# Four idle products in the opening, and the cumulated decays of both mixers by halves of the tokens

## The chip, the core and the metric

The program runs on one core of a Trainium2 chip. TensorE (PE, with its weight loads as PEld) multiplies into PSUM, VectorE (DVE), ScalarE (ACT) and GpSimd (POOL) work element by element, and SyncE (SP) issues most of the transfers from HBM. [...] The metric is the time of one execution in microseconds (us), the median of the runs.

## The reference, cut to what matters

A trunk of two layers works on 512 tokens of width 1024. Each layer modulates its input by a vector computed from `c` (adaLN), runs a mixer of gated linear attention and retention side by side, and then a channel mixer (dense in layer 0, eight experts in layer 1). The change touches the opening of layer 0, where the first modulation is made, and in both layers the cumulated decays `b` of the gated linear attention.

```python
cond = jax.nn.silu(c)
for layer in range(DEPTH):
    mod = (cond @ ada_w[layer] + ada_b[layer])[:, None, :]
    sh1, sc1, g1, sh2, sc2, g2 = jnp.split(mod, 6, axis=-1)
    h = rms_norm(x, norm_mix_g[layer]) * (1.0 + sc1) + sh1
    x = x + g1 * hybrid_mixer(h, positions, w_in[layer], ...)
    ...

def hybrid_mixer(h, ...):
    proj = (h @ w_in).astype(F32)
    gq, gk, gv, gr, ga, rq, rk, rv, rg = jnp.split(proj, ...)
    log_a = jax.nn.log_sigmoid(ga @ w_alpha + b_alpha) / GLA_TAU
    o_g = gla_core(gq * GLA_DK ** -0.5, gk, gv, log_a)      # in chunks of 64 tokens
    ...

def gla_core(q, k, v, log_a):
    b = jnp.cumsum(log_a, axis=2)
    b_last = b[:, :, -1:]
    eb, enb = jnp.exp(b), jnp.exp(-b)
    q_f, k_f = q * eb, k * enb
    q_b, k_b = q * enb, k * eb
    ...
```

## The kernel before, in words

Every weight matrix is read as f32 and split into two f16 halves (`split`: ACT writes `hi`, DVE writes `lo`), and every product of an activation with a weight is three f16 products (`mm3`, lines 221 to 223). The raw tiles stand in a ring of three buffers, the halves in rings of five.

**Opening (lines 1413 to 1438, `ada_first`).** The tokens are transposed (`px`), the scale of their norm is spread over the partitions (`prb`, line 400), and the scale and shift vectors of layer 0 are made from 8 MB of `ada_w`, in two halves of 512 columns, j = 1 (scale) before j = 0 (shift). A block of 128 rows of `ada_w` either goes through DVE, which adds it up in `acc` (lines 266 and 268), or through PE as a product with one column of output (`pr`, line 256), as the table `HOW` says. Products with one moving column bring the sum into columns (`pm`, lines 260 and 270), and DVE writes `mod` (line 273). From `mod` and the normalised tokens ACT makes `hh_m` and an f32 copy `u_m` (line 437), and DVE makes `hl_m` (line 438), for the eight blocks k of 128 features: blocks 0 to 3 need the first halves of scale and shift, blocks 4 to 7 the second ones.

**First products (`first`, lines 540 to 568).** For each k, PE multiplies into four banks of keys and queries (`pf_k`, `pf_q`) and into the bank of the gate's 16 columns (`pf_ga`, line 554). ACT then copies the four banks (`rawk`, `rawq`, line 568) and the gate (`gt`, line 560).

**The gate's chain (lines 560 to 607).** PE transposes `gt` into `pgt` (line 563), ACT copies it to `ga` (line 564), PE multiplies by the small matrix `wal` into two banks `pz`, one for each half of the tokens (line 578), ACT takes Abs, Exp and Ln of each (lines 582 to 586, with a load of the function table ahead of Exp and of Ln), and DVE makes the log decays, `es[0]` and `es[1]` (called `lge` in the trace, line 588), of 256 tokens each. Eight f32 products with a triangular matrix make the cumulated decays (`pbs`, line 596), and eight with two columns the chunks' ends (`pe`, line 597). ACT exponentiates them into `eb` and `enb`, which DVE needs for the keys and queries of the first step of the attention.

**Beside it.** `project_v` (line 510 on) makes the values `gv`: four tiles of 128 tokens, 24 f16 products each (96 in all, lines 221 to 223), which need nothing of the gate's chain. Also on ACT in this stretch: the sine and cosine of the rotary tables (`sinT`, `cosT`, lines 466 to 469) and the halves of later weights.

**What sets the order.** The program is written as straight code, but a scheduler of the framework decides the order of the instructions on each engine. PSUM has eight banks in two pools by tag: `at` with three, `pj` with five. During `first` all five `pj` banks are taken (four of keys and queries, one of the gate), and each tile of `gv` needs a `pj` bank. In the orders shown below, `pj` tiles are first written in the order in which the code asks for them.

Of the kernel before, what the change touches and what calls it, by code (L numbers as in the profile page):

```python
# [15 lines left out]
AF = mybir.ActivationFunctionType  # L16
ALU = mybir.AluOpType

P = 128
# [3 lines left out]
NT = T // P  # L23
# [95 lines left out]
def trunk(ctx, tc, a, out):  # L119
# [11 lines left out]
    def psum(name, tag="at", dt=F32):  # L131
        return ps_pool.tile([P, 512], dt, name=name, tag=tag, bufs=dict(at=3, pj=5)[tag])
# [20 lines left out]
    def scratch(name, dt=F32):  # L153
        return p1.tile([P, T], dt, name=name, tag="tmp", bufs=4)
# [73 lines left out]
    def ada_sum(l, j, c0, n, terms, scale):  # L228

        pm = psum(f"pm{l}_{j}_{c0}")  # L230
        for i in range(n // P):
            for m, (x, y) in enumerate(terms):
# [4 lines left out]
                                       (XS, 1.0, SCL)[j % 3] * scale, bcol[:, b0:b0 + n // P],  # L237
                                       op0=ALU.mult, op1=ALU.add)

    def ada_first(j, half, stage, how):  # L240

        if (0, j) not in mods:
            mods[0, j] = sb.tile([P, KC], F32, name=f"mod0_{j}")
        c0 = j * D + half * 512
        view, raw = kview(a["ada_w"][0][:, c0:c0 + 512]), []
        for i in range(2):
            r = stage.tile([P, 4, 512], F32, name=f"ada0_{j}_{half}_{i}", tag="ada", bufs=STG)
            last_dma[:] = [nc.sync.dma_start(r, view[:, i * 4:i * 4 + 4])]  # L250
            raw += [r[:, k] for k in range(4)]
        pm, acc, rows = psum(f"pm0_{j}_{half}"), None, [k for k in range(KC) if how[k] == "R"]
        if rows:
            pr = psum(f"pr0_{j}_{half}", "pj")[0:1]
            for k in rows:
                nc.tensor.matmul(pr, cond[:, k:k + 1], raw[k], start=(k == rows[0]), stop=(k == rows[-1]))
            row = scratch(f"row{j}_{half}")[0:1]
            nc.scalar.copy(row, pr)
            for i in range(4):
                nc.tensor.matmul(pm[:, i:i + 1], row[:, i * P:(i + 1) * P], ones[0:1, 0:1], start=(i == 0), stop=False)  # L260
        for k in range(KC):
            if how[k] == "V":
                c = cond[:, k:k + 1]
                if acc is None:
                    acc = stage.tile([P, 512], F32, name=f"acc{j}_{half}", tag="acc", bufs=2)
                    nc.vector.tensor_scalar(acc, raw[k], c, None, op0=ALU.mult)
                else:
                    nc.vector.scalar_tensor_tensor(acc, raw[k], c, acc, op0=ALU.mult, op1=ALU.add)
        for i in range(4):
            nc.tensor.matmul(pm[:, i:i + 1], acc[:, i * P:(i + 1) * P], ones[:, 0:1],  # L270
                             start=(not rows and i == 0), stop=(i == 3))
        b0, d0 = j * KC + half * 4, half * 4
        nc.vector.scalar_tensor_tensor(mods[0, j][:, d0:d0 + 4], pm[:, 0:4], (XS, 1.0)[j],
                                       bcol[:, b0:b0 + 4], op0=ALU.mult, op1=ALU.add)
# [214 lines left out]
    def mixer(l, hh, hl, ws, sp, ga_bank=None, tokens=None):  # L489
# [99 lines left out]
        la = [es[t // 2][:, (t % 2) * 256:(t % 2 + 1) * 256] for t in range(NT)]  # L589
        tri = con("tri")  # L590
        pe = psum(f"pe{l}")
        for p in range(2):
            pbs = psum(f"pbs{l}_{p}")
            for t in range(NT):
                w = la[t][:, p * P:(p + 1) * P]
                nc.tensor.matmul(pbs[:, t * P:(t + 1) * P], w, tri[:, 0:P], start=True, stop=True)
                nc.tensor.matmul(pe[:, p * 8 + 2 * t:p * 8 + 2 * t + 2], w, tri[:, P:P + 2],
                                 start=True, stop=True)
            nc.scalar.activation(eb[p], pbs, AF.Exp)
            nc.scalar.activation(enb[p], pbs, AF.Exp, scale=-1.0)  # L600
        ex = tl("ex", (P, 2, NT, 2))
        nc.scalar.activation(ex, pe[:, 0:16], AF.Exp)
        exx = tl("exx", (P, 2, NT - 1))
# [934 lines left out]
```

## Time and profile before

| | |
|---|---|
| median of 3 runs | 1371.9 us (1366.15 to 1373.17) |
| profiled execution, its own time | 1369.26 us |
| its span, first to last instruction | 1367.5 us |
| granted TensorE clock, mean | 0.984 |
| PE busy | 1318.8 us, 96% of the span |
| PEld / DVE / ACT / POOL busy | 924.9 / 1007.8 / 690.1 / 166.9 us |
| mean DMA rate | 205 GB/s |

The profiled execution lies 2.6 us below the median, and 1.8 us of it lie outside the span. A busy share is an average over stages, so what the change can give or take is read from the stretches that it touches: the first 95 us for layer 0, and the stretch from 660 to 690 us for layer 1. [...] In a row of the timeline the bracket at the end is the idle time of the engine just before, and what ended it; rows of one form that follow each other are merged.

### The profile page before, as it was taken

Reading aid. Unit: us, or ns where it says so; the run is one execution under the profiler, and the core shown is the slowest. Engines: PE = TensorE matmul, PEld = TensorE weight load, DVE = VectorE, ACT = ScalarE, POOL = GpSimd, SP = SyncE. Lnnn points to the kernel's source line nnn. Section 1 sums busy time; section 2 is a strip of 40 time slices with the busy share of each in tenths; the row PEclk is TensorE's granted clock in tenths of the full one; section 3 lists DMA queues with packets and bytes.
Section 4 is the critical chain, followed back from the end, with each engine's and each line's share of the span. In section 5 each row is a group of like instructions: output and inputs, shape, how many; then the busy total and the mean of one; then the engine's idle time right before and its main releaser. Section 6 shows DMA issues by size and latency. Waiting matters only on the chain.

```text
span 1367.5 us, 28435 instructions
## 1 busy us (share of the span) xinstructions
PE 1318.8 (96%) x11761; PEld 924.9 (68%) x11761; DVE 1007.8 (74%) x1823; ACT 690.1 (50%) x1107; POOL 166.9 (12%) x177
## 2 busy tenths in 40 slices
PE   5999999999999999999999999899999999999985
PEld 3455555574444444468655464599999999999983
DVE  6869977767778873236277875798988988978673
ACT  3762333444333432226632333577777877777563
POOL 1010100011122110002000401400000000000652
PEclk8999999999999999999999999999999999999997
DMA  9864643327768753324222200199999999989941
GB/s 343 287 205 135 206 134 101 114 63 218 247 226 294 229 189 116 111 82 139 94 93 92 68 1 1 35 379 383 360 312 353 360 308 364 361 290 353 318 155 64
DMA packets 163389, 279.78 MB, mean 205 GB/s; under 512 B 6224, under 2 KB 82012, under 8 KB 163252
## 3 DMA queue, kind: packets, MB, share of 16 engines
q1 hardware_dynamic: 149172, 229.01, 49.1%
q0 software_dynamic: 13936, 48.61, 10.9%
q8 instruction: 94, 1.54, 0.5%
q14 instruction: 43, 0.35, 0.1%
q10 hardware_dynamic: 144, 0.26, 0.1%
HBM read 271.80 MB, written 6.06 MB: 203 GB/s over the span
## 4 chain that ended last, share of the span: by engine, by line
PE 86%; DVE 6%; DMA 3%; ACT 2%; issue 1%; SPq 1%; POOL 0%; DVEq 0%; ACTq 0%; POOLq 0%
PE u L222 6%; PE u L223 6%; PE u L221 6%; PE eu L1176 5%; PE eu L1179 5%; PE eu L1177 5%; PE ed L1179 3%; PE ed L1177 3%; PE ed L1176 3%; PE pg L1198 2%; PE pd_None L223 2%; PE pd_None L222 2%; PE pd_None L221 2%; PE pj_gate L221 2%; PE pj_gate L222 2%; PE pj_gate L223 2%
## 5 line engine op out<-in xcount | busy, mean ns | idle before, releaser
L222 PE MATMUL u<-hl_f,hi_w 128*128 128x512 f16 (+1 forms) x384 | 137.5, 361 | 0.1
L223 PE MATMUL u<-hh_f,lo_w 128*128 128x512 f16 (+1 forms) x384 | 137.6, 361 | 0.0
L221 PE MATMUL u<-hh_f,hi_w 128*128 128x512 f16 (+1 forms) x384 | 135.2, 361 | 0.2 <-ACT hh_f L421 0.2
L203 ACT ACTIVATE hi_w<-raw_w 128x512 f16<-128x512 f32 (+1 forms) x136 | 72.9, 604 | 100.0 <-PE u L222 63.0
L204 DVE SCALAR_TENSOR_TENSOR lo_w<-raw_w,hi_w 128x512 f16<-128x512 f32 (+1 forms) x136 | 83.9, 671 | 37.2 <-ACT hi_w L203 37.0
L308 DVE SCALAR_TENSOR_TENSOR acc<-ada,conds,acc 128x512 f32<-128x512 f32 x140 | 104.9, 749 | 3.4 <-DMA ada<-in_ada_w 0.2
L294 POOL DMA_DIRECT2D ada<-in_ada_w x80 | 56.9, 712 | 347.8 <-DVE acc L308 320.9
L223 PEld LDWEIGHTS <-lo_w 128*128 128x128 f16 x604 | 59.1, 98 | 54.3 <-issue 0.3
L221 PEld LDWEIGHTS <-hi_w 128*128 128x128 f16 x604 | 59.2, 98 | 53.5 <-issue 0.2
L222 PEld LDWEIGHTS <-hi_w 128*128 128x128 f16 x604 | 59.0, 98 | 52.8
L1366 POOL DMA_INDIRECT y<-ybuf,rows x16 | 26.3, 1643 | 394.9 <-DMA raw_e7moe_w<-in_moe_w 388.8
L222 PE MATMUL pd_None<-al,hi_w 128*128 128x512 f16 x132 | 50.0, 379 | 0.0
L223 PE MATMUL pd_None<-ah,lo_w 128*128 128x512 f16 x132 | 50.0, 379 | 0.0
L221 PE MATMUL pd_None<-ah,hi_w 128*128 128x512 f16 x132 | 50.0, 379 | 0.0
L221 PE MATMUL pj_gate<-hh_m,hi_gate 128*128 128x512 f16 x128 | 48.5, 379 | 0.8 <-ACT g L766 0.8
L223 PE MATMUL pj_gate<-hh_m,lo_gate 128*128 128x512 f16 x128 | 48.5, 379 | 0.0
L222 PE MATMUL pj_gate<-hl_m,hi_gate 128*128 128x512 f16 x128 | 48.5, 379 | 0.0
L204 DVE SCALAR_TENSOR_TENSOR lo_e7moe_w<-raw_e7moe_w,hi_e7moe_w 128x2048 f16<-128x2048 f32 (+3 forms) x21 | 38.4, 1838 | 9.2 <-ACT hi_e7moe_w L203 6.3
L204 DVE SCALAR_TENSOR_TENSOR lo_e5moe_w<-raw_e5moe_w,hi_e5moe_w 128x2048 f16<-128x2048 f32 (+1 forms) x18 | 37.8, 2112 | 8.8 <-ACT hi_e5moe_w L203 8.6
L204 DVE SCALAR_TENSOR_TENSOR lo_e2moe_w<-raw_e2moe_w,hi_e2moe_w 128x2048 f16<-128x2048 f32 (+1 forms) x18 | 37.9, 2112 | 7.4 <-ACT hi_e2moe_w L203 7.1
L204 DVE SCALAR_TENSOR_TENSOR lo_e3moe_w<-raw_e3moe_w,hi_e3moe_w 128x2048 f16<-128x2048 f32 (+1 forms) x18 | 37.9, 2112 | 6.5 <-ACT hi_e3moe_w L203 6.3
L1198 PE MATMUL pg<-oneh,ht 128*128 128x284 f16 (+3 forms) x256 | 40.4, 295 | 2.1 <-DVE oneh L1191 2.1
(572 smaller groups left out, 4115.5 us busy)
## 6 DMA issues: line engine op xcount, KB each, us to landing
ada<-in_ada_w POOLq DMA_DIRECT2D x80, 512.0 KB, 5.0
raw_w<-in_ffn_w SPq DMA_DIRECT2D x26, 1024.0 KB, 6.5
raw_e1moe_w<-in_moe_w SPq DMA_DIRECT2D x12, 1024.0 KB, 8.0
raw_e2moe_w<-in_moe_w SPq DMA_DIRECT2D x12, 1024.0 KB, 6.5
raw_e3moe_w<-in_moe_w SPq DMA_DIRECT2D x12, 1024.0 KB, 8.1
raw_e4moe_w<-in_moe_w SPq DMA_DIRECT2D x12, 1024.0 KB, 7.4
raw_e5moe_w<-in_moe_w SPq DMA_DIRECT2D x12, 1024.0 KB, 7.1
raw_e6moe_w<-in_moe_w SPq DMA_DIRECT2D x12, 1024.0 KB, 7.4
```

Source lines behind the costliest of these rows:

```text
L203: nc.scalar.mul(hi, raw, WS)
L204: nc.vector.scalar_tensor_tensor(lo, raw, WS, hi, op0=ALU.mult, op1=ALU.subtract)
L221: nc.tensor.matmul(dst, wh, xh, start=first, stop=False)
L222: nc.tensor.matmul(dst, wh, xl, start=False, stop=False)
L223: last_mm[:] = [nc.tensor.matmul(dst, wl, xh, start=False, stop=last)]
L294: nc.gpsimd.dma_start(r, view[:, k:k + 2])
L308: op = nc.vector.scalar_tensor_tensor(acc, x, c, acc, op0=ALU.mult, op1=ALU.add)
L1176: nc.tensor.matmul(dst, wh[:, s], x1, start=(first and i == 0), stop=False)
L1177: nc.tensor.matmul(dst, wh[:, s], x2, start=False, stop=False)
L1179: nc.tensor.matmul(dst, wl[:, s], x1, start=False, stop=(last and i == len(ws) - 1))
L1198: nc.tensor.matmul(pg[:, 0:W], ht[j][t][d // 4][:, d % 4 * P:(d % 4 + 1) * P], oneh[:, t], start=(t == 0), stop=(t == NT - 1))
L1366: nc.gpsimd.indirect_dma_start(out=y, out_offset=None, in_=ybuf[half], in_offset=bass.IndirectOffsetOnAxis(ap=rows[:, i, t:t + 1], axis=0))
```

## The change

A function `idle` multiplies the identity by a tile of 512 columns in f32 and writes a `pj` bank that nobody reads. It is called four times, all in layer 0: on the finished `acc` of the first halves of scale and shift (`idle_a1`, `idle_a0`), on the last block of `ada_w` of the first row product (`idle_r0`), and on `es[0]` (`idle_g`). The products of the cumulated decays, which went through p (two groups of 128 channels) and in it through the four token tiles, now go through the halves of the tokens first, so that the first half of them reads `es[0]` alone; both `pbs` banks are asked for ahead of the loop, and the exponentials follow it. This holds for both layers; `idle_g` is called in layer 0 alone, between the halves.

```diff
+    def idle(name, x):
+
+        nc.tensor.matmul(psum(f"idle_{name}", "pj"), ident, x, start=True, stop=True)
+
     def ada_first(j, half, stage, how):
...
             for k in rows:
                 nc.tensor.matmul(pr, cond[:, k:k + 1], raw[k], start=(k == rows[0]), stop=(k == rows[-1]))
+            if half == 0:
+                idle(f"r{j}", raw[rows[-1]])
             row = scratch(f"row{j}_{half}")[0:1]
...
             nc.tensor.matmul(pm[:, i:i + 1], acc[:, i * P:(i + 1) * P], ones[:, 0:1],
                              start=(not rows and i == 0), stop=(i == 3))
+        if half == 0:
+            idle(f"a{j}", acc)
...
         pe = psum(f"pe{l}")
+        pbs = [psum(f"pbs{l}_{p}") for p in range(2)]
+        for j in range(2):
+            for p in range(2):
+                for t in (2 * j, 2 * j + 1):
+                    w = la[t][:, p * P:(p + 1) * P]
+                    nc.tensor.matmul(pbs[p][:, t * P:(t + 1) * P], w, tri[:, 0:P], start=True, stop=True)
+                    nc.tensor.matmul(pe[:, p * 8 + 2 * t:p * 8 + 2 * t + 2], w, tri[:, P:P + 2],
+                                     start=True, stop=True)
+            if l == 0 and j == 0:
+                idle("g", es[0])
         for p in range(2):
-            pbs = psum(f"pbs{l}_{p}")
-            for t in range(NT):
-                w = la[t][:, p * P:(p + 1) * P]
-                nc.tensor.matmul(pbs[:, t * P:(t + 1) * P], w, tri[:, 0:P], start=True, stop=True)
-                nc.tensor.matmul(pe[:, p * 8 + 2 * t:p * 8 + 2 * t + 2], w, tri[:, P:P + 2],
-                                 start=True, stop=True)
-            nc.scalar.activation(eb[p], pbs, AF.Exp)
-            nc.scalar.activation(enb[p], pbs, AF.Exp, scale=-1.0)
+            nc.scalar.activation(eb[p], pbs[p], AF.Exp)
+            nc.scalar.activation(enb[p], pbs[p], AF.Exp, scale=-1.0)
```

The scheduler orders much of layer 0 anew. Three places matter here. (Line numbers of the changed program are 4 to 12 higher.)

**PE, end of the first products of layer 0.** In the program before, the products of `gv` (`pv_gv`) follow the last product of the gate (`pf_ga`) directly:

```order
L554 MATMUL pf_ga_None<-gate_6_368,hh_m_400 128x32
L554 LDWEIGHTS hl_m_401
L554 MATMUL pf_ga_None<-gate_6_368,hl_m_401 128x32
L221 LDWEIGHTS hh_m_282
L221 MATMUL pv_gv_0_709<-hi_gv_0_687,hh_m_282 128x512
L222 LDWEIGHTS hh_m_282
L222 MATMUL pv_gv_0_709<-lo_gv_0_688,hh_m_282 128x512
```

The chain's own products `pgt` stood 31 products of `gv` further down, `pz` another 23 and `pbs` another 30. In the changed program:

```order
L562 MATMUL pf_ga_None<-gate_6_374,hl_m_407 128x32
L571 MATMUL pgt_None<-cst,gtNone_607 32x128 x4
L586 MATMUL pz_0_636<-wal_433,ga_437 128x256 x2
L586 MATMUL pz_1_637<-wal_433,ga_437 128x256 x2
L605 MATMUL pbs_0_653<-cst,lge_0_642 128x128
L606 MATMUL pe_652<-cst,lge_0_642 128x2
L605 MATMUL pbs_0_653<-cst,lge_0_642 128x128
L606 MATMUL pe_652<-cst,lge_0_642 128x2 x3
L242 MATMUL idle_g<-lge_0_642,cst 128x512
L221 LDWEIGHTS hh_m_288
L221 MATMUL pv_gv_0_717<-hi_gv_0_695,hh_m_288 128x512
```

The whole chain up to the first half of `pbs` and to `idle_g` now stands ahead of the first product of `gv`; the other products of `pbs` follow after twelve products of `gv`.

**ACT, the same stretch.** Before, from the last copies of the first products:

```order
L568 ACTIVATE rawq_0_615<-pf_q_None 128x512
L560 ACTIVATE gtNone_601<-pf_ga_None 128x128
L519 ACTIVATE gv_0_734<-pv_gv_0_709 128x512
L466 ACTIVATE sinT<-cosT 64x512
L467 ACTIVATE sinT<-cosT 64x512
L564 COPY ga_431<-pgt_None 32x512
L468 ACTIVATE cosT<-cosT 128x512
```

And in the changed program:

```order
L568 ACTIVATE gtNone_607<-pf_ga_None 128x128
L572 COPY ga_437<-pgt_None 32x512
L590 ACTIVATE lge_0_642<-pz_0_636 128x512
L474 ACTIVATE sinT<-cosT 64x512
L475 ACTIVATE sinT<-cosT 64x512
L592 ACT_TABLE_LOAD
L592 ACTIVATE lge_0_642<-lge_0_642 128x512
L476 ACTIVATE cosT<-cosT 128x512
L590 ACTIVATE lge_0_643<-pz_1_637 128x512
L594 ACT_TABLE_LOAD
L594 ACTIVATE lge_0_642<-lge_0_642 128x512
```

The copy `ga` and Abs follow `gt` directly, and two sines, one Abs of the cosine and the Abs of the second half stand inside the first half's chain.

**PE, the opening of layer 0.** Before, from the spread scale `prb` to the first product on `hh_m`:

```order
L400 MATMUL prb_m_0_186<-dg_m_0_185,cst 128x128 x4
L256 MATMUL pr_0_0_242<-ada_0_0_0_237,cond 1x512 x4
L180 MATMUL pv<-cst,rows_v 128x56
L183 MATMUL pb<-cst,rows_b 128x96
L270 MATMUL pm_1_0_209<-cst,acc_0_210 128x1 x4
L260 MATMUL pm_0_0_241<-cst,row_0_247 128x1 x4
L256 MATMUL pr_1_1_311<-ada_1_1_0_306,cond 1x512 x2
L270 MATMUL pm_0_0_241<-cst,acc_0_253 128x1 x4
L221 LDWEIGHTS hi_first_0_227
L221 MATMUL pf_k_None<-hh_m_282,hi_first_0_227 128x512
```

And in the changed program:

```order
L242 MATMUL idle_a_223<-acc_0_210,cst 128x512
L260 MATMUL pr_0_0_244<-ada_0_0_0_239,cond 1x512 x4
L242 MATMUL idle_r_249<-ada_0_0_0_239,cst 128x512
L180 MATMUL pv<-cst,rows_v 128x56
L183 MATMUL pb<-cst,rows_b 128x96
L276 MATMUL pm_1_0_209<-cst,acc_0_210 128x1 x4
L266 MATMUL pm_0_0_243<-cst,row_0_251 128x1 x4
L276 MATMUL pm_0_0_243<-cst,acc_0_257 128x1 x4
L242 MATMUL idle_a_266<-acc_0_257,cst 128x512
L260 MATMUL pr_1_1_317<-ada_1_1_0_312,cond 1x512 x2
```

Three idle products come in, and the product on the shift's `acc` goes ahead of the second row product. On DVE the writing of the first shift `mod` goes ahead of the last three steps of the next `acc`, and the four `lo_gv` of the second raw tile go ahead of the `hl_m` of block 4; on ACT the four `hi_gv` of that tile go ahead of the `hh_m` of block 4. In layer 1 the order around the chain keeps `gv` products between its steps; there the second part of the `pbs` products moves ahead by four products.

## Rows read from the trace of the kernel before

**Rows 1.** The page: busy us, share of the span and instructions, by engine.
```profile
PE 1318.8 (96%) x11761; PEld 924.9 (68%) x11761; DVE 1007.8 (74%) x1823; ACT 690.1 (50%) x1107; POOL 166.9 (12%) x177
```

**Rows 2.** The page: chain that ended last, shares of the span by engine.
```profile
PE 86%; DVE 6%; DMA 3%; ACT 2%; issue 1%; SPq 1%; POOL 0%; DVEq 0%; ACTq 0%; POOLq 0%
```

**Rows 3.** Waits of PE from 62 to 260 us: total, times, longest.
```profile
PE rpo L724 <- DVE rS L720: 1.7, 1, 1.7
```

**Rows 4.** Stretches: us, busy (count) of PE, PEld, DVE, ACT, POOL, clock, DMA, GB/s.
```profile
19.60:22.80 3.20, 3.20 (x10) 2.00 (x11) 3.20 (x9) 0.64 (x2) 0.00 (x0) 0.50 1.04 386
29.70:40.00 10.30, 7.75 (x21) 3.19 (x19) 10.19 (x21) 6.32 (x11) 0.00 (x0) 0.50 1.05 380
87.70:94.60 6.90, 6.90 (x24) 3.70 (x23) 5.44 (x11) 4.06 (x8) 0.00 (x0) 0.51 0.48 152
94.70:231.20 136.50, 135.71 (x779) 76.94 (x777) 114.36 (x307) 42.96 (x94) 11.38 (x16) 1.00 0.45 139
```

**Rows 5.** Timeline of PE in the opening: start, us, operation, tiles, form.
```profile
19.58 2.08 PE L400 MATMUL prb_m<-dg_m,cst 128*128 128x128 f32 x8 [5.19 <-DVE dg_m L399]
21.62 4.22 PE L256 MATMUL pr<-ada,cond 128*1 128x512 f32 x8
...
35.81 0.58 PE L221 MATMUL pf_k_None<-hh_m,hi_first 128*128 128x512 f16 x1 [1.28 <-ACT hh_m L437]
...
52.79 0.38 PE L222 MATMUL pf_k_None<-hl_m,hi_first 128*128 128x512 f16 x1
```

**Rows 6.** Timeline of DVE in the opening.
```profile
31.21 3.64 DVE L268 SCALAR_TENSOR_TENSOR acc<-ada,cond,acc 128x512 f32<-128x512 f32 x5
34.76 0.15 DVE L273 SCALAR_TENSOR_TENSOR mod<-pm,bcol 128x4 f32<-128x4 f32 x1
...
48.28 0.15 DVE L273 SCALAR_TENSOR_TENSOR mod<-pm,bcol 128x4 f32<-128x4 f32 x1
48.35 0.68 DVE L204 SCALAR_TENSOR_TENSOR lo_gv<-raw_gv,hi_gv 128x512 f16<-128x512 f32 x1
```

**Rows 7.** Timeline of PE from the end of the first products.
```profile
63.06 0.38 PE L221 MATMUL pv_gv<-hi_gv,hh_m 128*128 128x512 f16 x1
63.28 0.38 PE L222 MATMUL pv_gv<-lo_gv,hh_m 128*128 128x512 f16 x1
...
69.75 0.60 PE L563 MATMUL pgt_None<-cst,gtNone 128*32 128x128 f32 x4
75.24 1.99 PE L578 MATMUL pz<-wal,ga 33*128 33x256 f32 x8
86.03 0.49 PE L596 MATMUL pbs<-cst,lge 128*128 128x128 f32 x2 [1.43 <-DVE lge L588]
89.63 0.59 PE L221 MATMUL pv_gv<-hi_gv,hh_m 128*128 128x512 f16 x1
```

**Rows 8.** Timeline of ACT and DVE in the gate's chain.
```profile
63.10 2.19 ACT L203 ACTIVATE hi_rv<-raw_rv 128x512 f16<-128x512 f32 x4
65.67 0.27 ACT L560 ACTIVATE gtNone<-pf_ga_None 128x128 f32<-128x128 f32 x1
68.99 0.63 ACT L466 ACTIVATE sinT<-cosT 64x512 f32<-64x512 f32 x1
70.44 0.57 ACT L564 COPY ga<-pgt_None 32x512 f32<-32x512 f32 x1 [0.18 <-PE pgt_None L563]
76.41 0.60 ACT L582 ACTIVATE lge<-pz 128x512 f32<-128x512 f32 x1 [1.75 <-PE pz L578]
77.02 1.28 ACT L584 ACT_TABLE_LOAD   x1
78.32 0.63 ACT L584 ACTIVATE lge<-lge 128x512 f32<-128x512 f32 x1
80.75 0.63 ACT L586 ACTIVATE lge<-lge 128x512 f32<-128x512 f32 x1
81.41 0.69 DVE L588 SCALAR_TENSOR_TENSOR lge<-pz,lge 128x512 f32<-128x512 f32 x1 [1.95 <-ACT lge L586]
```

## The prediction

> **What bounds the kernel now.** I read the page first: PE is busy 96% of the span [rows 1], and the chain that ended last runs 86% over PE [rows 2]. So what costs PE time costs the kernel, unless a later wait takes it up. Then I looked for PE's waits behind the place of the change: from the end of the gate's chain to 231 us PE is busy for 135.7 of 136.5 us at full clock [rows 4], and the longest single wait in what follows is 1.7 us, on `rS` [rows 3], at the end of a chain that starts from PE's own products. A delay of PE at 65 to 95 us is therefore passed on nearly whole. [...] The fourth view is the timeline of PE, ACT and DVE at the two places where the order changes.
>
> **The gate's chain in layer 0 (the main term).** Before, the products of `gv` start at 63.06 us, one each 0.22 us (63.06 to 63.28), and hide the chain [rows 7]: while ACT and DVE make the log decays, PE does 84 of the 96. In the changed order `pgt`, `pz`, the first half of `pbs` and `idle_g` all stand ahead of `gv` on PE, and each of them but the last waits for the engine before it. What is queued behind the waiting products are the 96 products of `gv`, whose weights are there; who waits for that is everything PE does later. I count the chain from 63.06, with before's durations:
>
> - ACT is at the four `hi_rv` (63.10, 2.09 until the next copy), copies the last `rawq`, then `gt`, which ends at 65.67 + 0.27 = 65.94 [rows 8]. These stand in the same order in both programs.
> - `pgt` to the end of `ga`: 69.75 to 71.01 us, 1.26 [rows 7, 8]; so until 67.25.
> - `pz` to the end of Abs: 75.24 to 77.01, 1.77 [rows 7, 8]; with the hand-over until 69.07.
> - Two sines, now between, 0.63 each [rows 8]; until 70.35.
> - Table and Exp: 77.02 to 78.95, 1.93 [rows 8]; until 72.28.
> - Abs of the cosine and Abs of the second half, each taken at the 0.60 of Abs [rows 8]; until 73.5.
> - Table and Ln, the same forms, 1.93 (Ln ends at 80.75 + 0.63 [rows 8]); until 75.45.
> - DVE, 0.69 and a hand-over of 0.03 [rows 8]; until 76.17.
>
> So `pbs` can start 13.1 us after the point at which `gv` started. Of these PE itself needs 2.4 (`pgt` pushes the products beside it by 0.44, `pz` by 1.93 as the starts around them show; their 0.60 and 1.99 are pipelined lengths [rows 7]); **10.7 us** are an idle PE. Is there an escape? DVE and ACT are not late in this stretch: the cosine must be ready by 69 us, and DVE's order has it behind `lo_rv`, whose `hi_rv` ends at 65.2; four more operations of DVE at 0.4 to 0.7 us bring it to 67.5. Nothing on PE's queue can go ahead.
>
> A rule to weigh here: before, when `pbs` waited 1.43 us for `es[1]`, the last twelve products of `gv` stood ready behind it and none started before 89.63 [rows 7], so a waiting product holds all behind it. [...]
>
> **What the wait replaces.** Three other terms of this stretch:
> - Before's own wait of 1.43 us [rows 7] goes: the second half of `pbs` comes behind twelve products of `gv`. `es[1]` is ready some 5.8 us after `es[0]` (three tables at 1.28, the cosine, Exp and Ln at 0.63 each or a little more [rows 8]; DVE's step follows either), and until then PE does two `pbs`, four `pe`, `idle_g` and twelve products, 4.7 us at full clock by my estimate. With the low clock that I take next that wait is nil; at full clock it is about 1.
> - Before's low clock from 87.7 to 94.6 goes: 6.9 us at half speed [rows 4] cost 3.4.
> - A low clock comes in behind the new wait. PE was idle 5.19 us before 19.6 [rows 5], and then ran at half clock until 22.8, 3.2 us [rows 4]; from the first f16 products at 35.81 it took until 40.0, 4.2 us [rows 4, 5]. Half of that is lost: 1.6 to 2.1, at worst 3.4 as in the third stretch. I take **2.1**, the row with the same products.
> - `idle_g` itself: four row products of 512 columns took 4.22 us, 1.06 each [rows 5], partly at half clock; at full clock I estimate 0.9 (four times an f16 product's 0.22 [rows 7]). I take 0.9; its slower pass is in the term above.
>
> Sum of the stretch: 10.7 + 2.1 + 0.9 − 1.4 − 3.4 = **+8.9 us**.
>
> **The opening.** `idle_a1` puts the row product off by its own 0.9 and a wait for `acc` of about the same; the row product's reader is not urgent, since DVE has work until 34.8 [rows 6]. The useful part is the order on DVE: the first shift `mod`, at 34.76 behind five steps of `acc` at 0.73 each [rows 6], goes ahead of three of them, less small steps that stay: some 1.5 us earlier. `idle_a0` (0.9) and the row product (two at 1.06 [rows 5]) now lie between the sum and the first product on `hh_m`, which comes at about 34.9 instead of 35.81 [rows 5]. If the three idle products keep the clock up, the ten products until 40.0 save half of 4.2 us, 2.1. Together PE could be 3.1 us ahead. But it cannot keep that: the products of block 4 need `hl_m`, and its DVE has the same work ahead of the second `mod` (48.28 [rows 6]) plus one `lo_gv` at 0.60, less some 0.3 of idle time, then four more `lo_gv` (0.60 from start to start, [rows 6]) and `hl_m` itself: 48.6 + 2.4 + 0.15 + 0.6, about 51.8. Before, PE came to that product at 52.79 [rows 5], busy all the way. So the gain is 0 if the clock stays low, 3.1 if block 4 does not hold it, and I take **−0.9**.
>
> **Layer 1.** The chain there keeps its `gv` products; the second part of `pbs` moves ahead by four products of 0.22 us, and PE's list of waits shows none for `lge` there. Nothing: 0. If it came to wait, it would be for less than the four products that it moves, 0.9 us. The other reorderings move products among others on a PE that has no gaps there; the later exponentials are hidden by the products of the retention's keys (41 products, 9 us, stand before the first use of the scores).
>
> **The sum.** +8.9 − 0.9 = **+8.0 us**. The profiled execution took 1369.26 us, so 1377.3 on its footing; it lies 2.6 below the median of 1371.9, and on the median's footing the sum gives **1379.9**. I forecast 1380. From the ends (low clock 1.6 and opening 3.1 at one side, low clock 3.4 and opening 0 at the other) the change lies between +5.3 and +10.2: 1377 to 1382.
>
> **The rivals.**
> 1. **`gv` is not held** (not slower). If the products of `gv` pass the waiting chain, or the scheduler's banks let them through on the chip, the 10.7 us and the low clock fall away and the old wait and low clock go too: −0.9 + 0.9 − 1.4 − 3.4, −4.8, 1367. For it: nothing but that the waits of the idle products seem meant for PE's gaps. Against it: the 1.43 us [rows 7]. It decides from the point where PE idles less than 2.7 us in the chain (with the low clock of 2.1 behind it the sum is then below zero).
> 2. **The light case** (no change by the bound below). PE keeps its lead of 3.1 us in the opening, or the clock comes back fast behind the wait: +5.3 to +6.8, 1377 to 1378.7. For it: the clock in the opening rose in 3.2 us once [rows 4]. Against: DVE's order for block 4.
> 3. **Taken up later.** While PE idles, ACT and DVE run ahead; if this removes the waits of layer 0 that come later (`rS` 1.7 [rows 3] and the smaller ones of about 2 us in all), +8.0 becomes +4.3, 1376. Against: `rS` hangs on a chain that PE's own product starts.
> 4. **The heavy case.** The clock stays low as long as from 87.7 to 94.6 and the opening gains nothing: +10.2, 1382.
>
> **How the numbers follow.** A measurement of this kernel tells about 0.5% from no change, 6.9 us; the runs before spread by 7 us. Chances: the forecast (+6.9 to +9.5) 0.44, the heavy case 0.15, the light case 0.23, taken up later 0.11, `gv` not held 0.07. Slower by over 0.5%: 0.44 + 0.15, and a little less for the noise of two medians around a forecast that lies only 1.1 us above the bound: 0.56. Same: 0.23 + 0.11 + most of 0.07 + that little: 0.39. Faster: 0.05. The range takes in +5.3 to +10.2 and the spread of the medians on either side, and reaches to the case taken up later: 1372 to 1384.
>
> **What would show it.** Right: in the trace after, PE's first `pv_gv` product comes at 77 to 80 us instead of 63; between the last `pf_ga` and it PE shows three waits (ACT `gt` near 2.8 us, ACT `ga` under 1, DVE `lge` near 6.5); the granted clock is 0.50 for 3 to 5 us from `pbs` on; the first product of `pj_rk` comes at about 102 to 104 us instead of 94.65; behind it the two traces run apart by a constant. The first `pf_k` product stands near 35 and its clock is 1.00; block 4 begins with a wait for `hl_m` near 51. Wrong: `gv` products between `pz` and `pbs`, or a lead that shrinks between 100 and 300 us.

## The result, and the profile after

| | before | after |
|---|---|---|
| median of 5 runs | 1371.9 us (1366.15 to 1373.17) | 1382.52 us (1380.56 to 1383.2) |
| ratio, 95% interval | | 1.0089 [1.007, 1.0109] |
| profiled execution, its own time | 1369.26 us | 1382.52 us |
| its span | 1367.5 us | 1380.7 us |
| granted clock, mean | 0.984 | 0.978 |

The changed kernel is 10.6 us slower by the medians, 12.2 us by the ratio and 13.2 us by the two spans. The medians lie closest because the five runs of the kernel before spread over 7 us and their median is one of the upper three. The forecast was 8.0 us, and its bounds reached to 10.2. The page of the changed kernel, busy time by engine, answers to [rows 1]; the shares of the chain that ended last answer to [rows 2]:

```profile
PE 1325.7 (96%) x11769; PEld 927.5 (67%) x11769; DVE 1008.2 (73%) x1823; ACT 692.9 (50%) x1108; POOL 167.5 (12%) x177
...
PE 88%; DVE 6%; ACT 3%; DMA 2%; issue 1%; POOL 0%; SPq 0%; DVEq 0%; ACTq 0%
```

PE is busy 6.9 us longer, with eight records more: the four idle products, two passes each, are 7.2 us of busy time by themselves (2.04, 1.13, 1.93 and 2.05 us, below). The other 6.3 us of the span are idle time of PE.

**The gate's chain.** PE's waits between 60 and 120 us of the changed kernel (total, times, longest):

```profile
PE pbs L605 <- DVE lge L596: 6.1, 1, 6.1
PE pgt_None L571 <- ACT gtNone L568: 2.6, 1, 2.6
PE pz L586 <- ACT ga L572: 0.7, 1, 0.7
```

The forecast had about 6.5, 2.8 and under 1. The timeline of PE in this stretch (start, us, operation, tiles, form; the idle time just before in brackets) answers to [rows 7]:

```profile
63.63 0.18 PE L562 MATMUL pf_ga_None<-gate,hl_m 128*128 128x32 f16 x1
66.39 0.61 PE L571 MATMUL pgt_None<-cst,gtNone 128*32 128x128 f32 x4 [2.58 <-ACT gtNone L568]
67.72 3.69 PE L586 MATMUL pz<-wal,ga 33*128 33x256 f32 x8 [0.72 <-ACT ga L572]
77.51 0.80 PE L605 MATMUL pbs<-cst,lge 128*128 128x128 f32 x2 [6.10 <-DVE lge L596]
...
80.09 2.05 PE L242 MATMUL idle_g<-lge,cst 128*128 128x512 f32 x2
81.94 0.63 PE L221 MATMUL pv_gv<-hi_gv,hh_m 128*128 128x512 f16 x1
...
84.92 0.38 PE L222 MATMUL pv_gv<-lo_gv,hh_m 128*128 128x512 f16 x1
...
86.00 0.83 PE L605 MATMUL pbs<-cst,lge 128*128 128x128 f32 x6
...
106.57 0.72 PE L671 MATMUL pf<-qf,kf 64*128 64x128 f32 x8
107.12 0.61 PE L671 MATMUL pf<-rawq,rawk 64*128 64x128 f32 x8
107.67 0.39 PE L221 MATMUL pj_rk<-hh_m,hi_rk 128*128 128x512 f16 x1
```

The first product of `gv` starts at 81.94 instead of 63.06 us. The second part of `pbs` at 86.00 has no bracket: it waits for nothing. The stretches of the changed kernel, with the clock as the third column from the end, answer to [rows 4]:

```profile
30.00:40.00 10.00, 10.00 (x43) 4.62 (x42) 9.36 (x18) 6.13 (x12) 0.00 (x0) 0.83 1.06 379
40.00:63.00 23.00, 22.76 (x166) 12.45 (x165) 19.23 (x37) 18.28 (x33) 2.00 (x4) 1.00 0.73 241
66.00:78.00 12.00, 4.79 (x14) 3.21 (x15) 5.70 (x15) 8.85 (x13) 2.90 (x4) 0.58 0.94 327
78.00:84.00 6.00, 6.00 (x19) 3.48 (x19) 1.95 (x3) 4.58 (x6) 0.71 (x1) 0.50 0.41 127
84.00:87.00 3.00, 3.00 (x17) 1.88 (x16) 2.86 (x5) 0.00 (x0) 1.01 (x2) 0.85 0.20 26
87.00:106.00 19.00, 19.00 (x102) 9.38 (x102) 11.00 (x20) 7.65 (x14) 2.55 (x4) 1.00 0.31 98
285.00:305.00 20.00, 18.97 (x156) 16.07 (x154) 15.30 (x50) 8.87 (x22) 3.01 (x5) 0.91 0.14 47
```

`pgt`, right behind the wait for `gt`, still runs at full clock (1.00 from 66.4 to 67.7 us); for `pz` the clock is low (0.52 from 67.7 to 71.4 us), and it stays at 0.50 through the next wait, `pbs` and `idle_g` to about 84.7 us, where the spacing of the `gv` products goes from 0.43 to 0.22 us. The last row is a later fall of the clock, in the channel mixer, that the profile of before does not have:

```profile
285.00:305.00 20.00, 20.00 (x162) 15.68 (x161) 14.69 (x34) 11.65 (x29) 3.65 (x5) 1.00 0.18 54
```

**The opening.** The timeline of PE answers to [rows 5]:

```profile
22.88 2.04 PE L242 MATMUL idle_a<-acc,cst 128*128 128x512 f32 x2 [1.24 <-DVE acc L274]
24.86 4.58 PE L260 MATMUL pr<-ada,cond 128*1 128x512 f32 x8
29.37 1.13 PE L242 MATMUL idle_r<-ada,cst 128*128 128x512 f32 x2
...
33.56 1.93 PE L242 MATMUL idle_a<-acc,cst 128*128 128x512 f32 x2
35.41 2.71 PE L260 MATMUL pr<-ada,cond 128*1 128x512 f32 x4
38.06 0.39 PE L221 MATMUL pf_k_None<-hh_m,hi_first 128*128 128x512 f16 x1
...
53.38 0.38 PE L222 MATMUL pf_k_None<-hl_m,hi_first 128*128 128x512 f16 x1 [0.24 <-DVE hl_m L446]
```

From 22.88 to 53 us PE has no idle time, and it is PE's queue, not DVE, that now holds the first product on `hh_m`: 38.06 instead of 35.81 us [rows 5], though ACT had made the first `hh_m` by 35.0. From there its products run at full clock (0.22 us apart). At block 4 PE waits 0.24 us for `hl_m`: 53.38 instead of 52.79 us, 0.6 later, and the 0.6 stays: the last `pf_ga` product starts at 63.63 instead of 63.04.

**Where the two traces part.** Starts of products in us, from the two traces:

| | before | after | apart |
|---|---|---|---|
| last `pf_ga` | 63.04 | 63.63 | +0.6 |
| first behind `gv` (`pj_rk` before, `pf` after) | 94.65 | 106.57 | +11.9 |
| layer 0's mixer, first `po_None` | 236.1 | 246.2 | +10.1 |
| channel mixer's second matrix, first `pd` | 599.8 | 611.4 | +11.6 |
| experts' second matrix, last `ed` | 1265.4 | 1277.3 | +11.9 |
| span | 1367.5 | 1380.7 | +13.2 |

### The profile page after: what moved, and what is told of

It reads as the page before. It is cut to its first block, busy times and chain, and to the rows that moved or that the text cites. A ratio compares the mean times of both kernels' runs of the same rounds, so it can differ in the third digit from the quotient of the medians.

```text
span 1380.7 us, 28452 instructions
## 1 busy us (share of the span) xinstructions
PE 1325.7 (96%) x11769; PEld 927.5 (67%) x11769; DVE 1008.2 (73%) x1823; ACT 692.9 (50%) x1108; POOL 167.5 (12%) x177
## 4 chain that ended last, share of the span: by engine, by line
PE 88%; DVE 6%; ACT 3%; DMA 2%; issue 1%; POOL 0%; SPq 0%; DVEq 0%; ACTq 0%
PE eu L1188 6%; PE eu L1189 6%; PE eu L1191 6%; PE u L222 6%; PE u L223 6%; PE u L221 6%; PE ed L1191 3%; PE ed L1189 3%; PE ed L1188 3%; PE pg L1210 2%; PE pd_None L221 2%; PE pd_None L223 2%; PE pd_None L222 2%; PE pj_gate L221 2%; PE pj_gate L222 2%; PE pj_gate L223 2%
## 5 line engine op out<-in xcount | busy, mean ns | idle before, releaser
L204 DVE SCALAR_TENSOR_TENSOR lo_e0moe_w<-raw_e0moe_w,hi_e0moe_w 128x512 f16<-128x512 f32 (+2 forms) x30 | 39.3, 1333 | 4.3 <-ACT hi_e0moe_w L203 4.3
```

Source lines behind the costliest of these rows:

```text
L204: nc.vector.scalar_tensor_tensor(lo, raw, WS, hi, op0=ALU.mult, op1=ALU.subtract)
```

## The experiments

My theory was that one thing makes nearly all of the loss: `idle_g` asks for a `pj` bank (one of the five PSUM banks of that tag) ahead of `gv`, banks of a tag are given out in the order of asking, and so the chain that feeds `idle_g` stands ahead of the 96 products of `gv`. The rivals were that the split into halves does it by itself, that the idle product is dear in itself, and that the opening's idle products carry a good part. "First `gv`" below is the start of the first product of `gv` in the run's trace. Idle products change no output that is read.

### Which part carries the loss

**Without `idle_g`.**

```diff
-            if l == 0 and j == 0:
-                idle("g", es[0])
```

> The changed kernel without idle_g: the three idle products of the opening and the split into halves stay. Theory (bank order: the pj bank that idle_g asks for ahead of gv makes the whole gate's chain stand ahead of gv on PE): gv follows the last pf_ga product directly, near 63.6 us, PE has no wait for gt, ga or for the first lge, and what is left is the opening's +0.6 and a wait of some 1.4 us for es[1]: 1371 to 1374 us. Rival (the halves themselves pull the chain forward, idle_g costs no more than its own product of 2.05 us): first gv near 77, 1380 to 1381 us.

Measured: 1371.93 us (1369.91 to 1373.27), ratio to the kernel before 1.001 [0.9997, 1.0023]. The first `gv` product is back at 64.1 us, right behind the last `pf_ga` product, and of PE's waits between 60 and 120 us one is left:

```profile
PE pbs L605 <- DVE lge L596: 1.7, 1, 1.7
```

As the theory had it. The order in the trace says the same: without `idle_g`, `pgt` stands 31 products of `gv` down again.

**`idle_g` in another bank.**

```diff
             if l == 0 and j == 0:
-                idle("g", es[0])
+                nc.tensor.matmul(pe[:, 16:512], ident, es[0][:, 0:496], start=True, stop=True)
```

> The changed kernel, with idle_g writing into columns 16 to 511 of the bank of pe instead of a pj bank of its own; it still multiplies es[0], at the same place in the code. Theory (bank order): gv stands ahead of the chain again, first gv near 63.6 us; the idle product of 0.9 to 2.05 us falls into the wait for es[1], so between 0 and 1 us are added to the kernel without idle_g: 1371 to 1375 us. If the idle product keeps the clock up there, up to 3.4 us less than that. Rival (the idle product itself, by its wait for es[0], holds PE whatever bank it has): 1381 to 1383 us, first gv near 77.

Measured: 1371.78 us (1370.45 to 1374.47), ratio 1.0019 [1.0005, 1.0033]; first `gv` at 64.6. The idle product is still done, on the same input and at the same place of the code, and all but some 2.6 us of the loss (0.7 to 4.5 by the interval) is gone: it is the bank. Why the bank decides is argued, not shown: in all four kernels whose `idle_g` has a `pj` bank no product of `gv` stands ahead of it, and in the nine others 31 stand ahead of `pgt`, as the order of asking has it, but no run asks for the `pj` bank of `idle_g` behind `gv`. One thing was not as expected. The product does not fill the wait for `es[1]`, since the scheduler put it four products behind the waiting one (timeline of PE):

```profile
88.34 0.49 PE L605 MATMUL pbs<-cst,lge 128*128 128x128 f32 x2 [1.73 <-DVE lge L596]
...
89.25 1.08 PE L609 MATMUL pe<-lge,cst 128*128 128x496 f32 x2
```

**The halves alone**, with no idle product:

```diff
-            if half == 0:
-                idle(f"r{j}", raw[rows[-1]])
...
-        if half == 0:
-            idle(f"a{j}", acc)
...
-            if l == 0 and j == 0:
-                idle("g", es[0])
```

> The split into halves alone, with none of the four idle products. Theory (bank order): nothing in layer 0 moves but eight products among each other; a wait of about 1.4 us for es[1] stays, now with the first half of pbs ahead of it, as does the low clock behind it: 1371 to 1373 us, no change. Rival (the halves pull the chain forward): 1380 us.

Measured: 1369.79 us (1366.78 to 1374.04), ratio 1.0001 [0.9986, 1.0017], with the wait of 1.4 us for `es[1]` in its trace as before. To within some 2 us the halves cost nothing and bring nothing; that rival falls.

**Halves and `idle_g`, without the opening's idle products:**

```diff
-            if half == 0:
-                idle(f"r{j}", raw[rows[-1]])
...
-        if half == 0:
-            idle(f"a{j}", acc)
```

> The split into halves and idle_g in its pj bank, without the three idle products of the opening. Theory (bank order): the chain stands ahead of gv, with PE's three waits of 9 to 10 us in all, and low clock behind them; the opening is that of the kernel before, so 0.6 us less than the changed kernel: 1381 to 1383 us. Rival (a good part of the loss is the opening's idle products, which delay the first products by 2.3 us): 1376 to 1379 us.

Measured: 1380.32 us (1378.39 to 1383.3), ratio 1.0082 [1.0058, 1.0105]. Against the halves alone (1369.79) that is 10.5 us for `idle_g` in its `pj` bank. PE waits 3.3, 0.7 and 6.2 us in the chain, and the clock is 0.50 all the way from 66.6 to 87.0 us:

```profile
66.60:87.00 20.40, 13.52 (x37) 7.65 (x38) 7.03 (x16) 14.37 (x17) 3.74 (x6) 0.50 0.64 216
```

### The opening

**The three idle products alone**, in the kernel before:

```diff
+            if half == 0:
+                idle(f"r{j}", raw[rows[-1]])
...
+        if half == 0:
+            idle(f"a{j}", acc)
```

> The kernel before with the three idle products of the opening alone (the cumulated decays as before, no idle_g). By the prediction's step the opening gains 0.9 us: 1369 to 1370 us. By the trace of the changed kernel PE itself is late in the opening (first pf_k product near 38 instead of 35.8 us, at full clock from there), and the last pf_ga product ends 0.5 to 1.5 us later than in the kernel before: 1371 to 1373 us. Rival: the clock that they keep up outweighs it, last pf_ga near 61, 1368 us.

Measured: 1370.63 us (1367.67 to 1372.34), ratio 1.0002 [0.9989, 1.0014]. The first `pf_k` product starts at 37.4 us, the last `pf_ga` at 63.0. Neither the gain of the prediction nor a loss can be told from nothing.

**The same without `idle_a0`:**

```diff
-        if half == 0:
+        if half == 0 and j == 1:
             idle(f"a{j}", acc)
```

> The run before this, without idle_a0 (idle_a1 and idle_r0 stay). If the queue of PE is what delays the first product on hh_m, that product comes 1.7 to 2 us earlier than with idle_a0, near 36 us; what it does then is a matter of the clock: if idle_a0 is what keeps the clock up, the first products run at half clock until 40 or later and the last pf_ga product ends at the same time or up to 2 us later (1371 to 1374 us); if the clock comes back without it, the end is 1 to 2 us earlier (1369 to 1371 us).

Measured: 1370.22 us (1367.65 to 1371.17), ratio 1.0001 [0.9987, 1.0014]. The first product on `hh_m` comes 2.0 us earlier, with a wait for it, and its products run at half speed (0.43 us apart) until 38.3 (timeline of PE):

```profile
35.40 0.58 PE L221 MATMUL pf_k_None<-hh_m,hi_first 128*128 128x512 f16 x1 [1.73 <-ACT hh_m L445]
...
37.92 0.53 PE L222 MATMUL pf_q_None<-hl_m,hi_first 128*128 128x512 f16 x1
38.28 0.38 PE L223 MATMUL pf_q_None<-hh_m,lo_first 128*128 128x512 f16 x1
```

The last `pf_ga` product starts at 63.6, but this execution has a second low clock on the way (0.83 on the mean from 45 to 55 us, 1.00 in the run before), so the two traces do not show what `idle_a0` alone gives or takes. By the times it is nothing either way.

**How far one execution tells of the opening.** The kernel before, unchanged, profiled once more:

> The kernel before itself, a second profiled execution, to see how far the clock of the opening differs between executions of one program. If the low clock of the opening is set by the program, it is 0.50 from 30 to 40 us and nowhere else until 87, and the last pf_ga product starts near 63.0 us, as in the first. If it is not, a second low stretch between 47 and 55 us, as in five other kernels here that have this opening or one like it, moves that product to 65.5 to 66.6 us.

Measured: 1365.59 us. The clock is low from 28.6 to 38.8 us, one stretch of 10 us as in the first profile, and not low again before 86; the last `pf_ga` product starts at 62.0. So the two executions of the kernel before have the same opening, one us apart. But other kernels with the same order of products there do not share it: in the halves alone, in the two runs with `gv` ahead below and in the run just ahead of those two (halves, `idle_g` in the bank of `pe`) the clock was low from 34 or 35 to 41 or 42 us and then a second time behind 47, in a stretch in which PE had no gap. Just ahead of this second fall PE did the one-column products `pm` and the gate's products of 32 columns; it does the same in the kernel before, at full clock (1.00 from 45 to 50 us in both executions), with no fall behind it. The halves alone, by stretches:

```profile
34.00:41.00 7.00, 5.21 (x13) 1.78 (x13) 6.93 (x14) 6.08 (x9) 0.00 (x0) 0.52 1.05 384
45.00:55.00 10.00, 10.00 (x65) 6.13 (x64) 5.82 (x12) 6.99 (x12) 0.08 (x1) 0.66 0.76 239
```

Over the seven executions with the opening of before the last `pf_ga` product starts at 62.0, 63.0, 63.1, 65.7, 65.7, 66.4 and 66.6 us (mean 64.6), over the six with the three idle products at 63.0, 63.6, 64.1, 64.3, 64.6 and 67.0 (mean 64.4). A second low stretch is in four of the seven (0.66 or 0.83 on the mean from 45 to 55 us) and in two of the six (0.71, 0.83). What decides over it stays open.

### The low clock behind the wait

**Ten more products for nothing in the wait:**

```diff
         pe = psum(f"pe{l}")
+        if l == 0:
+            for i in range(10):
+                nc.tensor.matmul(pe[:, 16:512], hh[i % 8][:, 0:P], hh[i % 8][:, 0:496], start=True, stop=True)
```

> The changed kernel with ten more products for nothing, f16 of 496 columns on hh_m, into columns 16 to 511 of the bank of pe, between pz and pbs on PE: they fill 2.2 to 4.3 us of the wait of 6.1 us and delay nothing but themselves. Theory (the low clock behind the wait is worth some 3.6 us of the loss, and comes of the idle time): with less idle time the clock is back sooner, the last gv product ends 1 to 3 us earlier than 106.6, 1379 to 1381.5 us. Rival (the clock stays low whatever PE does in the wait, as it is low from pz on): no change from the changed kernel, 1382 to 1383 us.

Measured: 1378.13 us (1375.78 to 1382.1), ratio 1.0061 [1.004, 1.0082], 4.4 us below the changed kernel (3.8 by the two ratios). The ten products ran at half speed (4.22 us) and left 1.8 us of the wait; behind them the clock was 1.00, fell once more for 3.5 us and came back (stretches):

```profile
76.00:79.00 3.00, 1.27 (x12) 1.27 (x12) 1.84 (x3) 2.94 (x4) 0.00 (x0) 1.00 0.96 365
79.00:82.50 3.50, 3.50 (x9) 1.31 (x9) 0.00 (x0) 3.46 (x4) 0.72 (x1) 0.52 0.52 149
82.50:106.00 23.50, 23.50 (x138) 12.35 (x137) 16.85 (x28) 9.29 (x17) 3.90 (x6) 1.00 0.33 98
```

From the last `pf_ga` product to the first of `pj_rk` it takes 41.65 us instead of 44.04, 2.4 less, for work that is only added. So the idle time cost twice here: by itself, and by the clock behind it. The later fall of the clock near 293 us is missing in this execution as well: from `po_None` to `pd` it takes 363.6 us here and 365.2 in the changed kernel. Whether it is missing in the other five, and so makes up the rest of the 3.8 us, is not known.

### In search of a faster version

**Halves, with `idle_g` in the bank of `pe` and nothing in the opening:**

```diff
-            if half == 0:
-                idle(f"r{j}", raw[rows[-1]])
...
-        if half == 0:
-            idle(f"a{j}", acc)
...
-                idle("g", es[0])
+                nc.tensor.matmul(pe[:, 16:512], ident, es[0][:, 0:496], start=True, stop=True)
```

> The split into halves with idle_g in the bank of pe, and no idle products in the opening: the version that may be faster than both. In the second run here the clock stayed 1.00 from 88 to 96 us, where the kernels without idle_g have 0.57 to 0.8. If that is the idle product's doing, the stretch gains up to 3.4 us less its own 0.9, and the time is 1367 to 1369.5 us; if it was chance, 1369 to 1371 us, the time of the halves alone.

Measured: 1368.85 us (1363.25 to 1371.12), ratio 0.9984 [0.9968, 1.0]. The clock from 88 to 96 us is 0.61 here and 1.00 in the run above that has `idle_g` in the bank of `pe`, with the same products of `pbs`, `pe` and the idle one behind a wait for `es[1]` (1.4 us here, 1.7 there; rows of this run, then of the other):

```profile
88.00:96.00 8.00, 7.32 (x30) 5.46 (x31) 5.79 (x10) 6.51 (x12) 0.00 (x0) 0.61 0.49 163
...
88.00:96.00 8.00, 7.66 (x46) 4.95 (x47) 6.23 (x12) 7.32 (x15) 0.00 (x0) 1.00 0.43 131
```

So the idle product does not keep the clock up every time. Whether it sometimes does is not shown: the profiled execution is the slowest of the twelve, and three of them, at 1363.25 to 1364.43 us, lie below the fastest of the 29 runs of the kernel before beside them (1364.54).

**`gv` ahead of the cumulated decays**, in the kernel before:

```diff
+        if l == 0:
+            gv = project_v(C_GV, "gv")
         pe = psum(f"pe{l}")
...
-        gv = project_v(C_GV, "gv")
+        if l:
+            gv = project_v(C_GV, "gv")
```

> The kernel before with gv asked for ahead of the cumulated decays in the code of layer 0, so that all 96 products of gv, and not 84, stand ahead of pbs on PE. No idle product, no halves. Theory (in the kernel before the wait of 1.43 us for es[1] and the half clock of 6.9 us behind it cost 4.8 us together, and cover removes both): PE has no wait for lge, the clock stays 1.00, and the time is 2 to 5 us below the kernel before of the same chip. Rival (the low clock there comes of the f32 products, not of the wait): the wait goes but 3 us of half clock stay, 0 to 2 us gained. Rival (the exponentials come later by the twelve products and the first pf products wait for them): 0 to 2 us slower.

Measured: 1369.11 us (1366.84 to 1372.56), ratio 0.9986 [0.9974, 0.9997]. The wait for `lge` is gone from PE's list between 60 and 120 us, and so is the low clock (waits, then stretches):

```profile
PE pm L233 <- ACT acch L314: 0.7, 1, 0.7
PE pm L233 <- DVE accl L315: 0.2, 1, 0.2
...
86.00:96.00 10.00, 9.11 (x65) 5.89 (x64) 7.24 (x14) 9.93 (x17) 1.42 (x2) 1.00 0.34 97
```

All eight products of `pbs` are in that stretch, at 1.00: the f32 products alone did not bring the low clock there. From the last `pf_ga` product to `pj_rk` it takes 28.1 us instead of 31.6, 3.5 less, of the 4.8 that were to be had; 0.9 went to the two small waits above. At `po_None` 1.9 us of the 3.5 are left (171.2 against 173.1 us from the last `pf_ga` product), and the ratio says 1.9 us as well (0.4 to 3.6 by its interval). It is faster than the kernel before by 0.14%, at the edge of what can be told.

**The same edit in the kernel of the halves alone:**

> As the run before this, with the split into halves as well. With gv ahead nothing is left for the halves to cover; both theories expect the same time as the run before this within 1 us. If the halves were worth something by themselves, it is faster by the rest of the wait for es[1], up to 1.4 us.

Measured: 1368.93 us (1364.74 to 1373.66), ratio 0.9989 [0.9975, 1.0004]; 28.1 us in the same stretch. The halves add nothing that can be told.

### Products on 64 rows

The changed kernel gets 1.8 us back between `gv` and `po_None`. One piece is in the second step of the attention. The eight products `pf` of a step read 64 rows each, four of them the one half of the rows and four the other; each f32 product has two records in the trace, called passes here (16 for the eight products of a step). In the kernel before, the two groups of the second step stand apart (timeline of PE):

```profile
111.87 0.71 PE L659 MATMUL pf<-qf,kf 64*128 64x128 f32 x4
112.42 0.61 PE L659 MATMUL pf<-rawq,rawk 64*128 64x128 f32 x4
112.95 0.39 PE L222 MATMUL pj_rk<-hl_m,hi_rk 128*128 128x512 f16 x1
...
114.14 0.71 PE L659 MATMUL pf<-qf,kf 64*128 64x128 f32 x4
114.69 0.61 PE L659 MATMUL pf<-rawq,rawk 64*128 64x128 f32 x4
115.22 0.39 PE L221 MATMUL pj_rk<-hh_m,hi_rk 128*128 128x512 f16 x1
```

Each group of eight passes takes 1.08 us from start to the next start. In the changed kernel the halves alternate, and all sixteen passes take 1.10 us (106.57 to 107.67, above). To see whether it is the alternation:

```diff
-            for i, (k, q) in enumerate(((kf, qf), (kb, qb))):
-                for p in range(2):
-                    for o, pf in enumerate(pfs):
+            for o, pf in enumerate(pfs):
+                for i, (k, q) in enumerate(((kf, qf), (kb, qb))):
+                    for p in range(2):
```

> The changed kernel with the products of the attention's scores (pf, 64 rows each) written one row half after the other, four and four, instead of alternating. If products on different row halves run side by side only when they follow each other alternately, each step's eight products (sixteen passes) take 2.1 to 2.2 us instead of 1.1, 1 us more for each of the steps in which they stand together: 4 us in layer 0 and as much in layer 1 at most, 1384 to 1391 us. Rival (the sixteen passes took 1.1 us for another reason, such as their order in PSUM): 1.1 us again, 1382 to 1383 us.

Measured: 1381.92 us (1381.47 to 1387.27), ratio 1.0084 [1.0071, 1.0098]; the time does not tell it from the changed kernel. The timeline of the first step does:

```profile
109.31 0.71 PE L671 MATMUL pf<-qf,kf 64*128 64x128 f32 x4
109.86 0.27 PE L671 MATMUL pf<-rawq,rawk 64*128 64x128 f32 x1
109.86 0.37 PE L671 MATMUL pf<-qf,kf 64*128 64x128 f32 x1
...
110.41 0.61 PE L671 MATMUL pf<-rawq,rawk 64*128 64x128 f32 x4
110.95 0.39 PE L221 MATMUL pj_rk<-hh_m,hi_rk 128*128 128x512 f16 x1
```

Four and four take 1.64 us, neither the 1.10 of the alternation nor the 2.1 to 2.2 that I expected: the second group starts at 109.86, when half of the first is through, beside the rest of it (the `rawq` passes at 109.86 and behind). So here a later product on the other rows started ahead of earlier ones; the products of `gv`, on all 128 rows, did not in the changed kernel's wait of 6.10 us. And in these three kernels the products on different row halves ran side by side wholly when they alternated (1.10 us), by half when they followed each other four and four (1.64), not at all with other products between (2 × 1.08). In the kernel before that is worth about 1.06 us in its second step. The first step, in three pieces there (0.43, 0.65 and 0.43 us), takes 0.4 us more than in the changed kernel, the fourth 0.2 less (1.29 against 1.50). That is 1.3 of the 1.8 us; the other 0.5 stays open.

## Where the prediction was right and which steps failed

**Right: the place, the mechanism and the sign.** The chain holds `gv`; three waits of 2.6, 0.7 and 6.1 us stand where 2.8, under 1 and 6.5 were forecast; no `gv` product passes a waiting one; the second `pbs` does not wait. Four runs tie 10.5 us of the loss to the bank of `idle_g`. The first rival falls with the three waits. The products of `gv` were ready and did not pass: the split weights of `gv` were made by 52.7 us, `hh_m` and `hl_m` had served the products up to 63.63, ACT had emptied the `pj` banks by 66.3, and none of the 96 products started before 81.94. Rival 3 falls by the list of waits: PE's later ones are the same in both kernels (1.7 us on `rS`). Rival 4, to which I gave 0.15, is the one that came nearest.

**Failed: the sizes of three terms, each too low.** They are the low clock behind the new wait (2.1 forecast, 3.7 measured), the opening (−0.9 forecast, +0.6 measured) and the length of the chain (10.7 forecast, 11.5 measured). Together they make +11.9 us behind `gv` where the sum had +8.0. Term by term, for the two profiled executions:

| term | forecast | measured | how |
|---|---|---|---|
| chain until `pbs`, put down as idle PE | 10.7 | 11.5 | 77.51 − 63.65 = 13.86, less the same 2.4 |
| low clock behind the wait | 2.1 | 3.7 | see below |
| `idle_g` at full clock | 0.9 | 0.9 | 1.85 us at half clock, start to start |
| old wait, old low clock | −4.8 | −4.8 | neither is there |
| **the stretch** | **+8.9** | **+11.3** | |
| the opening | −0.9 | +0.6 | 63.63 − 63.04 |
| **behind `gv`** | **+8.0** | **+11.9** | 106.57 − 94.65 |

**The low clock.** From `pbs` at 77.51 until 84.92 everything ran at half speed: 2.58 us of `pbs` and `pe`, 1.85 of `idle_g`, 2.98 of seven `gv` products; half of these 7.4 us is 3.7. I had two rows to take it from, the 4.2 us of the opening's f16 products and the 6.9 us of `pbs` followed by `gv` [rows 4], and called the first "the row with the same products". It was the second that had them. With it the term would have been 3.4 and the sum +9.3. The run with `idle_g` and without the opening's idle products shows that even this was no upper bound: 20.4 us at 0.50 on the clock's row, of which PE was busy 13.5. My sign for this, half clock for 3 to 5 us from `pbs` on, came as 7.4.

**The chain's length.** PE stood idle for 9.4 of the 11.5 us; most of the rest is `pz`, which ran at half clock as well (3.69 us instead of the 1.99 of [rows 7]) behind the waits of 2.58 and 0.72 us. I had put the low clock behind the long wait alone; it came behind the first two. For the chain this is 0.85 us: from the start of `pz` to the Abs it takes 2.02 us instead of 1.17. A smaller slip: I had the cosine ready by 67.5 us. DVE ended it at 68.96 in the kernel before and at 70.54 in the changed one, where ACT waited 0.23 us ahead of the first sine. The first `gv` product so came at 81.94, not between 77 and 80.

**The opening** failed in its own step: I let the first product on `hh_m` follow DVE, at 34.9, and priced the idle products at 0.9 each. At half clock (0.50 and 0.54) `idle_a1` and `idle_a0` took 2.0 and 1.9 us, and the row products behind them 4.6 and 2.7, in part at half clock (0.78 and 0.68 on the mean); PE itself became the late one, and the product came at 38.06. What I had right is that the clock then gives most of it back (2.25 us late at that product, 0.6 at block 4), and that block 4 waits for `hl_m`; but the second `mod`, behind the late PE, came at 50.16 instead of 48.6, and so this wait ended at 53.38 instead of 51.8. The runs do not resolve the sign of the whole: the ratio of the three products alone is 1.0002, and the means over all traces are 64.4 and 64.6.

**Behind `gv`** the lead was to stay constant, and to shrink between 100 and 300 us was my sign of being wrong. It did shrink, by 1.8 us until `po_None`, and 1.5 go again in the channel mixer, so that it is luck that the 11.9 us still stand at `ed`. The 1.5 are a fall of the clock, to 0.91 on the mean from 285 to 305 us in the changed kernel. It stands right behind two waits at the start of the channel mixer, 0.77 and 0.18 us, which all fourteen traces have at that place, and four of the fourteen show the fall (365.2 or 365.3 us from `po_None` to `pd`, 363.6 or 363.7 in the others): the changed kernel, the run with `idle_g` alone, the run with the row halves apart, and the run with `gv` ahead and halves, which has no held chain. Why it falls in these four is not shown. The last 1.3 us of the 13.2 lie behind the last `ed` product; from there to the last `pc` product it takes 85.6 to 89.7 us over the fourteen traces, with no order by kernel (88.2 and 85.7 in the two of before, 89.7 after). So they are this execution's, and the 12.2 us of the ratio lie nearer to the 11.9 at `ed`.

**Layer 1**: no new wait, as forecast; between 620 and 750 us both lists of PE's waits hold one of 0.7 us, for `hh_m`.

## What to carry to other kernels

A product that nobody reads still asks for a bank, and the bank can set the order of the engine: here one idle product cost 10.5 us by the bank that it took, and at most a few us in another. Filler belongs in a bank that the work beside it doesn't need. Moving real work that is ready into the wait (`gv` ahead of `pbs`, ratio 0.9986) took the wait of 1.43 us and the low clock (0.51 from 87.7 to 94.6 us before, 1.00 from 86 to 96 with the edit) away without added work, though by the times it is no better than halves and filler in the bank of `pe` (0.9984). And the idle PE had two prices in the changed kernel: 9.4 us of waits, and 3.7 us by the low clock of what followed, which I should have taken from the row whose products are the same as those that follow. Not every wait had the second: behind the one of 1.73 us in the changed kernel with `idle_g` in the bank of `pe` the clock was 1.00 (88 to 96 us).

## What the runs showed of the hardware that I had not expected

The granted clock fell in a stretch in which PE had no gap: to 0.66 on the mean over 45 to 55 us in the halves alone, where PE was busy for 10.00 of 10 us, with low clock ahead of it at 34 to 41 us (0.52), full clock from 41 to 47 (1.00), and one-column and 32-column products just before the fall. Of the seven executions with the same order of products in the opening the four with this second fall start their last `pf_ga` product at 65.7 to 66.6 us, the three without at 62.0 to 63.1. And f32 products on the two 64-row halves ran side by side: sixteen passes in 1.10 us alternating, 1.64 four and four, 2 × 1.08 with other products between.
